# Batched attention-times-value: TensorE's program rewritten as a loop over units, with the spreading of v moved ahead of the unit's transposes

## The chip, the cores and the metric

The kernel runs on one NeuronCore of one Trainium2 chip. The metric is the device time of one execution in microseconds (us). A core has five engines with their own instruction streams: TensorE (PE, its weight loads are shown apart as PEld), VectorE (DVE), ScalarE (ACT), GpSimd (POOL) and SyncE (SP). They meet only at semaphores. Sixteen DMA engines move data between HBM and the on-chip memory; POOL and SP issue the transfers here. An engine's sequencer (PEq, SPq and so on in the profile) handles waits, branches and register arithmetic.

## The reference

```python
batch, n_heads, seq, head_dim = 8, 12, 1024, 64
...
def reference(attn_weights, v):
    return np.einsum('bhqs,bhsd->bhqd', attn_weights, v).astype(np.float32)
```

For each of 96 heads a 1024 x 1024 matrix of float32 is multiplied with a 1024 x 64 matrix. The sum runs over s, the last axis of `attn_weights`, while a matrix product on TensorE sums over partitions. So every block of `attn_weights` has to be transposed first.

## The kernel before

Heads are taken four at a time: q counts 24 such groups (`NV`). Partition 32h + p holds 32 query rows of head h of the group. Each group is cut into two units of 16 rows for each partition, so there are 48 units (`NU`); unit 2q + i lives in the buffer `abf[i]`, one of two. POOL loads a unit with one transfer that casts float32 to bf16 on the way (`load_attn`, L344). The load of unit n + 2 goes into the buffer of unit n, and POOL issues it once unit n's transposes are done. POOL also loads v for four groups at a time (`load_v`, L350), and stores part of the output in two bursts in mid-run and one at the end (L358); SP stores the last groups. All of POOL's transfers lie in one software queue in the order of their issue.

TensorE does four things for a unit:

- 16 groups (g) of four transposes each (`transpose_g`, L144) into four PSUM banks in turn. VectorE and ScalarE copy a group to `at` (`copy_g`, L277), ten groups by VectorE and six by ScalarE. Group g waits for the copy of group g - 4 (`s_cp`); the second eight wait for `s_half`, which SP raises and which holds units back only behind the bursts of stores and, in the last two units, until the second half of the load has landed.
- In even units, the spread (`spread_v`, L161): 32 matmuls of 512 columns, eight for each of the group's four heads, with a 0/1 matrix as weights, which distribute v (`vr`) over the partitions in the order the product needs. They write all of `po` and `px`, four PSUM banks. VectorE and ScalarE copy them to `vbf` (`spread_copy`, L250). Head h has its v in 16 partitions, and the matmuls read a block of 32 partitions; heads 0 and 1 are in one block, 2 and 3 in another, and the heads are taken in pairs (0, 2) and (1, 3), matmul by matmul in turn.
- The transposes back of the unit before (`transpose_back`, L174, eight matmuls from `ot` into `px`), which ScalarE copies to `osb` (`back_copy`, L258).
- The product (`multiply`, L189): 64 matmuls into `po`, which VectorE and ScalarE copy to `ot` half each (`product`, L289).

The order on TensorE is written out by hand. Its loop has 24 turns of two units each, and the body holds the product twice, the transposes twice, the transposes back twice, and the spread four times, one copy for each place that v can have in `vr`, chosen by three branches. VectorE and ScalarE loop over four units. In `unit` the copies of the transposes stand first, then (even units) the two spread copies of the engine, then, on ScalarE, the copies back, then the product's copy.

SP waits at the start until both halves of the first v are there. The second half is issued by POOL behind the load of unit 0 (L367); SP's wait for it shows in the profile at L413. Then it raises `s_vr`, on which the spread waits.

Of the kernel before, what the change touches and what calls it, by code (L numbers as in the profile page):

```python
# [10 lines left out]
def kernel(  # L11
# [76 lines left out]
    def count_of(g):  # L88

        return sum(on_dve(x) == on_dve(g) for x in range(g + 1))  # L90

    PER_DVE = sum(on_dve(g) for g in range(G))
    PER_ACT = G - PER_DVE

# [27 lines left out]
    s_t = {True: sem("s_t_dve"), False: sem("s_t_act")}  # L122
# [4 lines left out]
    s_last, s_ot, s_vbf = sem("s_last"), sem("s_ot"), sem("s_vbf")  # L127
# [8 lines left out]
    with tc.tile_critical(sync_engine=mybir.EngineType.Pool, no_gpsimd_drain=True):  # L136
        pe = nc.tensor

        def transpose_g(a, g, n):
            if g >= 4:  # L140
                pe.wait_ge(s_cp[g - 4], n)
            words = a[:, g].bitcast(fp32).rearrange("p (c k) -> p k c", k=KW)
            for k in range(KW):
                last = pe.matmul(  # L144
                    out=pt[g % 4][:, k],
                    lhsT=words[:, k],
                    rhs=ident,
                    is_transpose=True,
                    start=(k == 0),
                    stop=(k == KW - 1),  # L150
                )
            last.then_inc(s_t[on_dve(g)])

        def spread_v(n, banks):

            for pair in ((0, 2), (1, 3)):
                for b in range(VB):
                    for h in pair:
                        j = n % 2 * VH + h
                        rows = ds(j * (P // V8) // VR * VR, VR)  # L160
                        last = pe.matmul(  # L161
                            out=banks[h],
                            lhsT=spread[rows, j, ds(VB - 1 - b, P)],
                            rhs=vr[rows, n // 2, b],
                            start=(b == 0),
                            stop=(b == VB - 1),
                        )
                        if b == VB - 1:
                            last.then_inc(s_sp)

        def transpose_back():
            for j0 in range(0, GH, 4):
                for j in range(4):
                    last = pe.matmul(  # L174
                        out=px[j0 // 4][:, ds(j * P, P)],
                        lhsT=ot[:, j0 + j],
                        rhs=ident,
                        is_transpose=True,
                        start=(j == 0),
                        stop=(j == 3),  # L180
                    )
                last.then_inc(s_back)

        def multiply(outs, h, half):

            n = 0
            for kw in range(KW):
                for par in range(2):
                    last = pe.matmul(  # L189
                        out=outs,  # L190
                        lhsT=vbf[:, 2 * kw + par, h],
                        rhs=at[:, ds(half * GH, GH), kw, ds(h * VP, VP), par],
                        start=(n == 0),
                        stop=(n == SB - 1),
                    )
                    n += 1
            return last

        def pe_unit(i, n, both, loaded, it):

            pe.wait_ge(*loaded)
            for g in range(G):
                if g == GH:
                    pe.wait_ge(s_half, n)
                transpose_g(abf[i], g, n)
            pe.wait_ge(s_ot, both)
            if i == 0:
                pe.wait_ge(s_vr, it)
                which = pe.snap((it - 1) % V_AT_ONCE)
                with pe.If(which > 1):  # L210
                    with pe.If(which > 2):
                        spread_v(3, po + px)
                    with pe.Else():
                        spread_v(2, po + px)
                with pe.Else():
                    with pe.If(which > 0):
                        spread_v(1, po + px)
                    with pe.Else():
                        spread_v(0, po + px)
                pe.wait_ge(s_vbf, it * 4)  # L220
            transpose_back()
            pe.wait_ge(s_last, both)
            for hp in range(2):
                for h in range(2):
                    for half in range(2):
                        outs = po[hp][ds(half * D, D), ds(h * GH * VP, GH * VP)]
                        last = multiply(outs, 2 * hp + h, half)
                last.then_inc(s_m)

        pe.wait_ge(s_const, 4)  # L230
        with nc.Fori(1, NV + 1, 1, engines=(PE,)) as it:
            loaded = pe.snap(it * 16)
            second = pe.snap(it * 2)
            first = pe.snap(second - 1)
            both = pe.snap(it * 4)
# [230 lines left out]
```

## Time and profile before

| | us |
|---|---|
| median of 3 runs (lowest to highest) | 1050.49 (1050.24 to 1050.53) |
| the profiled execution's own time | 1050.36 |
| its span, first to last instruction | 1049.0 |
| PE busy / DVE busy / ACT busy | 794.9 / 389.5 / 469.6 |
| PE idle ahead of the transposes (L144) | 211.2, of it 187.8 until a load of `abf` had landed |
| mean granted clock of TensorE | 0.875 of full speed |

The profiled execution is 0.13 us under the median, and 1.36 us of its time lie outside the span. In the profile, "busy" is the union of an engine's instructions; a row like "9.45 PE bank L144 x64" in the chain of waits is a piece of the path that ended last, with its start in front. In the timeline a row holds start, duration, engine, line, operation, output from inputs, count, and in brackets how long the engine was idle before and what released it. DMA share is the mean busy share of the 16 DMA engines; it is summed from whole packets, so a short stretch can read above 1.

### The profile page before, as it was taken

What the parts mean: (1) busy time and instruction counts of PE and PEld (TensorE: products, weight loads), DVE (VectorE), ACT (ScalarE), POOL (GpSimd) and SP (SyncE); (2) the same over time, 40 slices, a digit from 0 to 9 for tenths busy, and PEclk for the clock granted to TensorE, in tenths of its full rate; (3) what the DMA queues carried; (4) which work ended last, traced back from release to release, by engine and by line L of the source; (5) the groups of instructions that cost most, each with busy time, mean ns of one, the idle gap of its engine ahead of it and who ended that gap; (6) DMA issues with size and microseconds to landing.
All of it is one profiled execution on the core that took longest, in us unless ns stands there. A gap on an engine that the chain in (4) does not pass through costs nothing.

```text
span 1049.0 us, 17363 instructions
## 1 busy us (share of the span) xinstructions
PE 794.9 (76%) x7304; PEld 708.4 (68%) x7304; DVE 389.5 (37%) x584; ACT 469.6 (45%) x590; POOL 36.9 (4%) x68
## 2 busy tenths in 40 slices
PE   0978788479889393888949789758678884987994
PEld 0777687368778383777838688657667774867884
DVE  1443344234435151343515344323324332533542
ACT  0445355244545261354525455344435543544553
POOL 1000000000000000000000000000000000000000
PEclk9989799798999696889969899887878987998998
DMA  9999999999999999999999999999999999999999
GB/s 216 225 219 219 217 211 215 220 219 217 220 216 210 218 220 379 217 220 210 211 223 219 219 219 220 203 220 220 318 236 220 212 211 223 219 220 215 212 214 400
DMA packets 10662, 239.68 MB, mean 228 GB/s; under 512 B 1056, under 2 KB 1056, under 8 KB 1184
## 3 DMA queue, kind: packets, MB, share of 16 engines
q0 software_dynamic: 10080, 232.26, 98.9%
q1 hardware_dynamic: 576, 7.34, 1.7%
q8 instruction: 3, 0.05, 0.0%
q14 instruction: 3, 0.02, 0.0%
HBM read 427.82 MB, written 25.17 MB: 432 GB/s over the span
## 4 chain that ended last, share of the span: by engine, by line
DMA 71%; PE 26%; issue 1%; POOL 1%; ACT 0%; DVE 0%; ACTq 0%; SPq 0%; POOLq 0%
DMA abf<-in_attn_weights_dram 63%; PE bank L144 22%; DMA out_dram<-osb 8%; PE bank L161 3%; PE bank L189 1%; PE bank L174 0%; POOL vr L350 0%; ACT osb L258 0%; DVE osb L258 0%; ACT vbf L250 0%; POOL abf L344 0%; ACT ot L289 0%; POOL out_dram L358 0%; ACTq L258 0%; SPq L420 0%
## 5 line engine op out<-in xcount | busy, mean ns | idle before, releaser
L144 PE MATMUL bank<-ident,abf 128*128 128x128 f32 x3072 | 431.0, 308 | 211.2 <-DMA abf<-in_attn_weights_dram 187.8
L144 PEld LDWEIGHTS bank<-ident,abf 128*128 128x128 f32 x3072 | 421.3, 212 | 222.9 <-DMA abf<-in_attn_weights_dram 195.5
L277 DVE COPY at<-bank 128x1024 bf16<-128x1024 bf16 x480 | 319.7, 689 | 402.2 <-PE bank L144 395.5
L277 ACT COPY at<-bank 128x1024 bf16<-128x1024 bf16 x288 | 287.9, 1012 | 329.1 <-PE bank L144 329.1
L189 PE MATMUL bank<-at,vbf 128*64 128x256 bf16 x3072 | 225.2, 285 | 0.0
L189 PEld LDWEIGHTS bank<-at,vbf 128*64 128x64 bf16 x3072 | 203.4, 111 | 19.0 <-issue 6.1
L258 ACT COPY osb<-bank 64x512 f32 (+1 forms) x194 | 112.4, 580 | 28.2 <-PE bank L174 25.6
L289 DVE COPY ot<-bank 128x512 f32<-128x512 f32 x48 | 33.2, 692 | 207.1 <-PE bank L189 207.1
L161 PE MATMUL bank<-vr,spread 32*128 32x512 bf16 x768 | 87.0, 375 | 0.5 <-issue 0.2
L289 ACT COPY ot<-bank 128x512 f32<-128x512 f32 x48 | 28.1, 585 | 129.0 <-PE bank L189 129.0
L174 PE MATMUL bank<-ident,ot 128*128 128x128 f32 x392 | 61.6, 309 | 29.3 <-ACT vbf L250 28.7
L174 PEld LDWEIGHTS bank<-ident,ot 128*128 128x128 f32 x392 | 50.7, 158 | 41.4 <-ACT vbf L250 40.5
L161 PEld LDWEIGHTS bank<-vr,spread 32*128 32x128 bf16 x768 | 35.2, 93 | 43.9 <-issue 1.6
L250 ACT CAST vbf<-bank 128x512 bf16<-128x512 f32 x48 | 25.8, 589 | 74.3 <-PE bank L161 74.3
L344 POOL DMA_DIRECT2D abf<-in_attn_weights_dram x50 | 26.9, 537 | 814.8 <-PE bank L144 813.9
L250 DVE CAST vbf<-bank 128x512 bf16<-128x512 f32 x48 | 30.9, 686 | 29.0 <-PE bank L161 29.0
L277 ACT ACT_TABLE_LOAD x12 | 15.4, 1283 | 6.4 <-DMA osb<-in_v_dram 6.2
L350 POOL DMA_DIRECT2D vr<-in_v_dram x6 | 4.0, 674 | 134.6 <-PE bank L161 134.6
L358 POOL DMA_DIRECT2D out_dram<-osb x5 | 3.1, 620 | 7.5 <-ACT osb L258 7.5
L258 DVE COPY osb<-bank 64x512 f32<-64x512 f32 x2 | 1.4, 689 | 3.0 <-PE bank L174 3.0
L325 DVE MEMSET ident<- 128x128 f32 x1 | 0.2, 165 | 6.2 <-DMA osb<-in_v_dram 6.2
L332 DVE CAST vr<-osb 128x1024 bf16<-128x1024 f32 x2 | 2.2, 1138 | 0.0
(9 smaller groups left out, 5.1 us busy)
## 6 DMA issues: line engine op xcount, KB each, us to landing
abf<-in_attn_weights_dram POOLq DMA_DIRECT2D x46, 4096.0 KB, 29.1
vr<-in_v_dram POOLq DMA_DIRECT2D x5, 2048.0 KB, 15.8
out_dram<-osb POOLq DMA_DIRECT2D x1, 8192.0 KB, 39.4
abf<-in_attn_weights_dram POOLq DMA_DIRECT2D x4, 2048.0 KB, 22.9
out_dram<-osb POOLq DMA_DIRECT2D x3, 2048.0 KB, 32.9
out_dram<-osb SPq DMA_DIRECT2D x3, 2048.0 KB, 14.2
out_dram<-osb POOLq DMA_DIRECT2D x1, 4096.0 KB, 41.7
osb<-in_v_dram SPq DMA_DIRECT2D x1, 1024.0 KB, 5.1
```

The lines of the kernel that those rows point to most:

```text
L144: last = pe.matmul(out=pt[g % 4][:, k], lhsT=words[:, k], rhs=ident, is_transpose=True, start=(k == 0), stop=(k == KW - 1),)
L161: last = pe.matmul(out=banks[h], lhsT=spread[rows, j, ds(VB - 1 - b, P)], rhs=vr[rows, n // 2, b], start=(b == 0), stop=(b == VB - 1),)
L174: last = pe.matmul(out=px[j0 // 4][:, ds(j * P, P)], lhsT=ot[:, j0 + j], rhs=ident, is_transpose=True, start=(j == 0), stop=(j == 3),)
L189: last = pe.matmul(out=outs, lhsT=vbf[:, 2 * kw + par, h], rhs=at[:, ds(half * GH, GH), kw, ds(h * VP, VP), par], start=(n == 0), stop=(n ...
L250: copy(out=vbf[:, :, h], in_=ps.rearrange("p (k d) -> p k d", k=SB)).then_inc(s_vbf)
L258: last = copy(out=rows[ds(n // 2 % 2 * HP, HP), ds(pp * 2 * G + n % 2 * G, G)].rearrange("p (half j) d -> p j half d", half=2)[:, ds(4 * k ...
L277: ins = copy(out=at[:, g].rearrange("c k j two -> c (k j two)"), in_=bank[g % 4].bitcast(bf16),)
L289: copy(out=ot.rearrange("c j (pp h p) -> c h j pp p", pp=2, h=VH)[:, ds(2 * e, 2)], in_=po[e].rearrange("c (h j p pp) -> c h j pp p", h=2, ...
L332: last = nc.vector.tensor_copy(out=vr_first[:, 0, part], in_=v32[:, part])
L344: pool.dma_start(out=abf[n % 2][:, ds(g0, gn)].rearrange("p g s -> p (g s)"), in_=attn_q[n // 2][:, ds((n % 2 * G + g0) * S, gn * S)],).th ...
L350: pool.dma_start(out=vr[:, ds(q % V_AT_ONCE // 2, fours // 2)].rearrange("p n b x -> p n (b x)"), in_=v_n(q, fours),).then_inc(s_v, 16)
L358: eng.dma_start(out=out_n(q, fours), in_=at_slot, **({"single_packet": True} if eng is pool and fours == 2 else {}),).then_inc(done, 16)
```

## The change

TensorE now loops over units: 49 turns (`NU + 1`), each of which runs the product of the unit before, then the transposes of this unit, then the transposes back. The first turn has no product, the last no transposes. There is one copy of the product, one of the transposes back, and one of the transposes for each of the two buffers, chosen by a branch. What was the product at the end of a unit is now at the head of the next turn, so the order of transposes, transposes back and product is the same as before.

The spread stands in front of the even unit's transposes, after the product of the unit before, and has one copy: a loop over the four heads with eight matmuls in each turn, whose addresses come from registers (the bank, the head's place in `spread`, the half of `vr`). The matmuls read all 128 partitions, not a block of 32. The spread waits for both copies of the product before (`s_ot`), because it writes the same `po`; and the even unit's transposes wait in the program behind it. The last transposes of an even unit wait for the spread copies (`s_vbf`), instead of the transposes back.

PE, the end of an even unit's transposes and what followed, before (the rows `x32` are the copies of the spread):

```order
L144 MATMUL bank<-ident,abf 128x128 [waits s_cp11]
L144 MATMUL bank<-ident,abf 128x128 x3
L206 ISA
L210 ISA [waits s_vr,s_ot]
L210 COMPARE_AND_BRANCH
L211 COMPARE_AND_BRANCH
L161 MATMUL bank<-vr,spread 128x512 x32
```

The spread came after the last transposes of its unit (those that wait for `s_cp11`). Now, on PE, the start of an even unit:

```order
L153 UNCONDITIONAL_BRANCH [waits s_ot1,s_vr,s_ot0,s_const]
L153 ISA
L155 ISA x2
L155 MATMUL bank<-vr,spread 128x512
L155 ISA
L155 MATMUL bank<-vr,spread 128x512
L155 ISA
L155 MATMUL bank<-vr,spread 128x512
```

and the end of the spread's loop with the transposes behind it:

```order
L155 MATMUL bank<-vr,spread 128x512
L153 REGISTER_ALU
L153 COMPARE_AND_BRANCH
L210 ISA
L142 MATMUL bank<-ident,abf 128x128 [waits s_abf0]
L142 MATMUL bank<-ident,abf 128x128 x15
L142 MATMUL bank<-ident,abf 128x128 [waits s_cp0]
```

So the first transpose of an even unit (it waits for the load, `s_abf0`) now stands behind the spread, and each spread matmul behind a register instruction.

VectorE's loop has two units instead of four, and both engines' spread copies stand at the head of an even unit. VectorE, around the spread copies, before:

```order
L277 COPY at<-bank 128x1024 [waits s_t_dve]
L249 ISA
L250 CAST vbf<-bank 128x8x64 [waits s_sp] x2
L288 REGISTER_ALU
L289 COPY ot<-bank 128x2x16x16 [waits s_m]
```

and now:

```order
L287 ISA
L227 CAST vbf<-bank 128x8x64 [waits s_sp]
L226 REGISTER_ALU
L227 CAST vbf<-bank 128x8x64 [waits s_sp]
L253 REGISTER_ALU
L254 COPY at<-bank 128x1024 [waits s_t0]
L254 COPY at<-bank 128x1024 [waits s_t2]
```

The two casts went from behind the unit's last copy to ahead of its first. The semaphores for transposed groups are counted by bank (`s_t0` to `s_t3`) rather than by copying engine. POOL issues the same transfers in the same order; it waits for `s_t3`, which the last group raises, and for the spread's count.

```diff
-    bank = [nc.alloc_psum_tensor(f"bank{i}", [P, 512], fp32).ap() for i in range(8)]
-    pt = [b.rearrange("p (k j) -> p k j", k=KW) for b in bank[:4]]
-    po = bank[4:6]
-    px = bank[6:8]
+    bank = nc.alloc_psum_tensor("bank", [P, 8, 512], fp32).ap()
+    pt = [bank[:, i].rearrange("p (k j) -> p k j", k=KW) for i in range(4)]
+    po, px = (bank[:, ds(i, 2)] for i in (4, 6))
...
+        def transposes(i, n):
+            for g in range(G):
+                if g >= 4:
+                    pe.wait_ge(s_cp[g - 4], n)
+                words = abf[i][:, g].bitcast(fp32).rearrange("p (c k) -> p k c", k=KW)
+                for k in range(KW):
+                    if g == GH - 1 and k == KW - 1:
+                        pe.wait_ge(s_half, n)
+                    if i == 0 and g == G - 1 and k in (1, 2):
+                        pe.wait_ge(s_vbf[k - 1], n)
+                    last = pe.matmul(
...
+                last.then_inc(s_t[g % 4])
-        def spread_v(n, banks):
-
-            for pair in ((0, 2), (1, 3)):
+        def spread_v(j0, part):
+            with nc.Fori(0, VH, 1, engines=(PE,)) as h:
                 for b in range(VB):
-                    for h in pair:
-                        j = n % 2 * VH + h
-                        rows = ds(j * (P // V8) // VR * VR, VR)
-                        last = pe.matmul(
-                            out=banks[h],
-                            lhsT=spread[rows, j, ds(VB - 1 - b, P)],
-                            rhs=vr[rows, n // 2, b],
...
+                    last = pe.matmul(
+                        out=bank[:, ds(h + 4, 1)].rearrange("p one x -> p (one x)"),
+                        lhsT=spread[:, ds(h + j0, 1), ds(VB - 1 - b, P)].rearrange(
+                            "p one x -> p (one x)"
+                        ),
+                        rhs=vr[:, ds(part, 1), b].rearrange("p one x -> p (one x)"),
+                        start=(b == 0),
+                        stop=(b == VB - 1),
+                    )
+                last.then_inc(s_sp, 2)
...
+        def multiply(it):
+            for h in range(VH):
+                for half in range(2):
...
+                            if h == 0 and (half, n) in ((0, SB - 1), (1, 0)):
+                                pe.wait_ge(s_last[half], it)
...
+        def step(it):
+            with pe.If(it > 1):
+                multiply(it)
+            with pe.If(it < NU + 1):
+                with pe.If(pe.snap(it % 2) < 1):
+                    pe.wait_ge(s_abf[1], pe.snap(it * 8))
+                    transposes(1, it)
                 with pe.Else():
...
+                    pe.wait_ge(s_const, 4)
+                    for e in range(2):
+                        pe.wait_ge(s_ot[e], it)
+                    pe.wait_ge(s_vr, it)
+                    spread_v(pe.snap(it // 2 % 2 * VH), pe.snap(it // 4 % 2))
+                    pe.wait_ge(s_abf[0], pe.snap(it * 8 + 8))
+                    transposes(0, it)
+            for e in range(2):
+                pe.wait_ge(s_ot[e], it)
             transpose_back()
...
+        with nc.Fori(1, NU + 2, 1, engines=(PE,)) as it:
+            step(it)
...
+                now = [base + (4 * n + c) for c in range(9)]
+                if n % 2 == 0:
+                    spread_copy(e, po[:, e], now[2 * e + 2])
+                    spread_copy(2 + e, px[:, e], now[2 * e + 6]).then_inc(s_vbf[e], 2)
                 for g in mine:
-                    copy_g(g, of_t + (n * per + count_of(g)))
-                if n % 2 == 0:
-                    spread_copy(e, po[e], of_sp + (2 * n + 2 * e + 2))
-                    spread_copy(2 + e, px[e], of_sp + (2 * n + 2 * e + 2))
+                    copy_g(g, now[g // 4 + 1])
...
-            un = 4
+            un = 2 if dve else 4
...
-                pool.wait_ge(s_sp, 4 * (q + 1))
+                pool.wait_ge(s_sp, 8 * (q + 1))
                 load_v(q + 1, V_LOADS[q + 1])
-            pool.wait_ge(s_t[True], (n + 1) * PER_DVE)
+            pool.wait_ge(s_t[3], 4 * (n + 1))
             load_attn(n + 2)
```

More of the change, by code (lines that the diff above doesn't have):

```diff
@@ L120 @@
     s_held = sem("s_held")
-    s_t = {True: sem("s_t_dve"), False: sem("s_t_act")}
+    s_t = [sem(f"s_t{b}") for b in range(4)]
     s_sp, s_m = sem("s_sp"), sem("s_m")
@@ L137 @@
         pe = nc.tensor
[L139 to L152, printed above, removed]
@@ L181, in transpose_back @@
                     )
[L182 to L197, printed above, removed]
@@ L230 @@
[L230 to L235, printed above, removed]
-            pe_unit(0, first, pe.snap(both - 2), (s_abf[0], loaded), it)
-            pe_unit(1, second, both, (s_abf[1], loaded), it)
-        pe.wait_ge(s_ot, 2 * (NU + 1))
-        transpose_back()
+                last.then_inc(s_back, 2)
+        def multiply(it):
+            for h in range(VH):
+                for half in range(2):
+                    n = 0
+                    for kw in range(KW):
+                        for par in range(2):
+                            if h == 0 and (half, n) in ((0, SB - 1), (1, 0)):
+                                pe.wait_ge(s_last[half], it)
+                            last = pe.matmul(
+                                out=po[ds(half * D, D), h // 2, ts(h % 2, GH * VP)],
+                                lhsT=vbf[:, 2 * kw + par, h],
+                                rhs=at[:, ds(half * GH, GH), kw, ds(h * VP, VP), par],
+                                start=(n == 0),
+                                stop=(n == SB - 1),
+                            )
+                            n += 1
+                last.then_inc(s_m)
```

86 lines of the change are left out of this document (29 added, 57 removed).

## The prediction

> **What bounds the kernel now.** I read the page's parts on the DMA queues first, then the costliest groups, then the windows cut at places where the DMA rate changes, and last the timeline at both ends.
>
> ```profile
> DMA  9999999999999999999999999999999999999999
> ...
> q0 software_dynamic: 10080, 232.26, 98.9%
> q1 hardware_dynamic: 576, 7.34, 1.7%
> q8 instruction: 3, 0.05, 0.0%
> ...
> L144 PE MATMUL bank<-ident,abf 128*128 128x128 f32 x3072 | 431.0, 308 | 211.2 <-DMA abf<-in_attn_weights_dram 187.8
> ```
>
> ```profile
> 0.00:4.70 4.70, 0.00 (x0) 0.00 (x0) 0.00 (x0) 0.00 (x0) 1.95 (x7) 1.00 0.61 202
> 4.70:25.00 20.30, 0.00 (x0) 0.00 (x0) 4.20 (x6) 1.28 (x1) 2.25 (x2) 1.00 1.01 219
> 25.00:48.00 23.00, 20.53 (x168) 17.26 (x168) 8.62 (x13) 9.99 (x13) 0.58 (x1) 0.93 1.04 223
> 48.00:400.00 352.00, 273.96 (x2568) 245.20 (x2568) 135.06 (x203) 164.95 (x207) 11.73 (x21) 0.89 1.01 217
> 400.00:1022.00 622.00, 487.91 (x4441) 434.49 (x4442) 233.88 (x351) 284.17 (x357) 20.37 (x37) 0.86 1.01 228
> 1022.00:1047.00 25.00, 12.46 (x129) 11.48 (x127) 7.71 (x12) 9.15 (x13) 0.00 (x0) 0.86 0.99 418
> 1047.00:1049.00 2.00, 0.00 (x0) 0.00 (x0) 0.00 (x0) 0.00 (x0) 0.00 (x0) 0.50 0.18 74
> ```
>
> Columns of the windows: stretch, its length, busy time of PE, PEld, DVE, ACT and POOL, granted clock, DMA share, GB/s. The DMA share is about 1 from 4.7 to 1047 us: in loads at 217 to 228 GB/s, at the end in stores at 418. The software queue alone is busy for 98.9% of the span. PE idles 211.2 us ahead of the transposes, 187.8 of it for a load. So the time is 4.7 us, plus the bytes at these rates, plus 2 us. The change moves no bytes, so TensorE can only matter where it lets the queue run dry, or at the two ends.
>
> The queue runs dry if the load of unit n + 2, issued after unit n's transposes, comes later than the last data of load n + 1. The steady pace:
>
> ```profile
> 88.20 7.95 PE L144 MATMUL bank<-ident,abf 128*128 128x128 f32 x64
> 95.99 1.04 PE L174 MATMUL bank<-ident,ot 128*128 128x128 f32 x8
> 96.95 4.48 PE L189 MATMUL bank<-at,vbf 128*64 128x256 bf16 x64
> 110.74 9.81 PE L144 MATMUL bank<-ident,abf 128*128 128x128 f32 x64 [9.30 <-DMA abf<-in_attn_weights_dram]
> ...
> 149.35 9.34 PE L144 MATMUL bank<-ident,abf 128*128 128x128 f32 x64 [3.81 <-DMA abf<-in_attn_weights_dram]
> ```
>
> Two loads take 149.35 - 110.74 = 38.6 us, 19.3 each. A unit without its spread takes 96.95 + 4.48 - 88.20 = 13.2 us on PE when it starts without a pause, and transposes after a pause take 9.3 to 9.8 us instead of 7.95.
>
> **The spread's price.** It loses its pairs.
>
> ```profile
> L161 PE MATMUL bank<-vr,spread 32*128 32x512 bf16 x768 | 87.0, 375 | 0.5 <-issue 0.2
> ...
> L210 PEldq FUSED_REGOPS  x24: 67/69/80, 34.5 to 1009.1; - x24
> ...
> L231 PEldq COMPARE_BRANCH  x24: 67/208/218, 60.0 to 1032.7; - x24
> ```
>
> 768 matmuls fill 87.0 us, 113 ns each, while one of them lasts 375 ns: they overlap. Two neighbours lie in different blocks of partitions and write different banks, so I read 113 as half of a 227 ns step of a pair. Matmuls over all 128 partitions that add into one bank have no such neighbour. The trace has none of 512 columns. Bounds: 113 ns (3.6 us for a spread, if pairing gave nothing) and 375 ns (12.0 us, no overlap at all). I take 227 ns, 7.3 us, since it is one pass of 512 columns in the same trace. A register instruction of 69 ns ahead of each hides under 227. The loop's four branches of 0.2 us hide in PE's queue: at PE's old loop end the next transposes start after 0.20 us of idle, no later than where there is no branch (the row at 88.20 has no gap at all).
>
> The Trainium skill speaks against this part: its page "TensorE: Matmul & The Clock Gate", section "Why this matters for your kernels", says that a matmul over 32 partitions takes as long as one over 128 and that the gain is in running several row blocks at once. That gain is what the change gives up, and the 113 ns agree with it. The same page (Part 1) gives 215.7 ns for 512 columns at full clock; by that a spread is an estimated 6.9 us, and the sum below comes out 0.4 us earlier at the first load.
>
> **Steady state: nothing.** An odd unit now is followed by the spread before the even unit's transposes. The spread waits for ScalarE's copy of the product:
>
> ```profile
> 1034.79 1.09 PE L174 MATMUL bank<-ident,ot 128*128 128x128 f32 x8 [0.68 <-ACT ot L289]
> ...
> 76.58 3.63 PE L161 MATMUL bank<-vr,spread 32*128 32x512 bf16 x32
> ...
> 80.27 1.07 ACT L250 CAST vbf<-bank 128x512 bf16<-128x512 f32 x2 [3.07 <-PE bank L161]
> 80.53 0.53 POOL L350 DMA_DIRECT2D vr<-in_v_dram  x1 [23.57 <-PE bank L161]
> 81.06 0.54 POOL L344 DMA_DIRECT2D abf<-in_attn_weights_dram  x1
> 81.40 1.56 PEld L174 LDWEIGHTS bank<-ident,ot 128*128 128x128 f32 x8 [1.68 <-ACT vbf L250]
> ```
>
> From an odd load's landing PE needs 13.2 + 0.7 + 0.4 (a branch, three register instructions) + 7.3 = 21.6 us to the even transposes, 29.6 to their end; with a slow start of the odd ones (1.9) 31.5. The next landing is due at 38.6. So POOL issues the load 7 us before the queue needs it, where it had about 10: covered. Per pair PE needs 2 x 13.2 + 1.1 + 7.3 = 34.8 of 38.6 us. If this cover goes, the queue stops once in each pair.
>
> What else moves is free by the same cover. PE's wait for `vbf` (last row, 1.68 us for PEld) goes; next is the wait for the load. The spread copies now stand ahead of the transposes' copies; at the spread's end ScalarE has one left (0.53 us), and the second group, its first, needs two groups' time, 1.0 us. POOL's load of v (six times) was issued after the spread and held back the load of `abf` by 4.4 us (81.06 against 76.6, where the transposes had ended and the spread began); now v goes out while the transposes run, and the queue's order is the same. VectorE's twelve more loop ends cost some 0.1 us each on an engine busy 37%.
>
> **The start: here it is decided.**
>
> ```profile
> 0.74 0.38 SPq L134 DMA_DIRECT2D osb<-in_v_dram  x1
> ...
> 1.33 0.67 POOL L344 DMA_DIRECT2D abf<-in_attn_weights_dram  x1 [0.89 <-POOLq L450]
> 2.00 0.55 POOL L367 DMA_DIRECT2D vr<-in_v_dram  x1
> ...
> 25.20 9.90 PE L144 MATMUL bank<-ident,abf 128*128 128x128 f32 x64 [25.20 <-DMA abf<-in_attn_weights_dram]
> ...
> 35.40 0.58 POOL L344 DMA_DIRECT2D abf<-in_attn_weights_dram  x1 [25.23 <-PE bank L144]
> ...
> 48.19 2.07 PE L144 MATMUL bank<-ident,abf 128*128 128x128 f32 x15 [1.03 <-DMA abf<-in_attn_weights_dram]
> ```
>
> ```profile
> L413 SPq EVENT_SEMAPHORE  x1: 16884/16884/16884, 10.7 to 10.7; - x1
> ```
>
> Unit 0's transposes began at 25.20, when load 0 had landed. Now the first spread stands ahead, and its v lands behind load 0: SP's wait ends at 10.7 + 16.9 = 27.6. Branch and register instructions: 28.0. The spread starts on an idle PE; the first transposes took 9.90 instead of 7.95, so I add 2.0 to 7.3: it ends at 37.3. The transposes then run warm, 7.95: 45.2. POOL issues load 2 some 0.3 later (35.40 against 35.10 before): 45.5, 10.1 us later than before. Load 1 had landed at 48.2. The margin is 2.7 us, and in it the new load must get its first data moving.
>
> ```profile
> 1.00:1.50 0.50, 0.00 (x0) 0.00 (x0) 0.00 (x0) 0.00 (x0) 0.17 (x1) 1.00 0.00 0
> 1.50:2.00 0.50, 0.00 (x0) 0.00 (x0) 0.00 (x0) 0.00 (x0) 0.50 (x2) 1.00 1.02 180
> ...
> 4.50:5.00 0.50, 0.00 (x0) 0.00 (x0) 0.00 (x0) 0.00 (x0) 0.00 (x0) 1.00 3.15 819
> ```
>
> SP's transfer (0.74) moves data from 1.5 to 2.0 on: 0.8 to 1.3 us. POOL's first (1.33) was there at the latest when the rate jumped at about 4.7: 3.4 us. With 0.8 to 1.3 first data flow at 46.3 to 46.8, ahead of the landing by 1.4 or more, and the queue does not stop; with 3.4 they flow at 48.9, a stop of 0.7. I take the middle, 0.4 us. Bounds: a spread at 113 ns leaves 6 us of margin, stop 0; at 375 ns plus 3.4 us first data come at 53.7, a stop of 5.5. A stop is paid in full, since nothing later has slack in the queue.
>
> **The end.**
>
> ```profile
> 1024.72 4.11 PE L144 MATMUL bank<-ident,abf 128*128 128x128 f32 x32 [0.75 <-SPq L426]
> 1024.79 12.88 SPq L358 DMA_DIRECT2D out_dram<-osb  x3
> ...
> 1037.34 0.33 SPq L358 DMA_DIRECT2D out_dram<-osb  x1
> ```
>
> After the last load five stores of 2.1 MB remain; at 418 GB/s they fill the 25 us to 1047. The four earlier ones last to about 1042, and the last is issued at 1037.3. So PE may be up to some 3 us later there for nothing. It gets one transpose more after the last landing (0.12) and two branches (0.4).
>
> **Sum.** 1050.36 + 0.4 + 0 = 1050.8; the profiled execution is 0.13 under the median: 1050.9. A gain can hardly exceed 1.2 us: the queue never stops, and the shorter program saves at most the three instruction packets, each 0.05 MB / 3 = 17 KB, or 1.2 us on one DMA engine (219 / 16 GB/s), which a load waits for if it is the last one.
>
> **Rivals.** (1) Slower, the other side: the first spread is dearer or POOL's first data later, and the queue stops before load 2. Each us by which the transposes end later than 46.6 (44.5, if POOL's first data take 3.4 us) costs one; 0.2% (2.1 us, about what a measurement of this kernel can tell from no change) is reached 2.1 us after that. With 300 ns a matmul (register addresses) they end at 47.6, and with 3.4 us of delay the queue stops for 3.1: 1053.6; the bound is 1056.0. For it: the thin margin; against: 227 ns and SP's delay. (2) The spread is so dear in every pair that PE becomes the bound. Five loads of v (9.6 us each) lengthen the mean pair to 40.6, so the spread must exceed 40.6 - 27.5 = 13.1 us, 410 ns a matmul, over the 375 that one lasted. At half clock, 14.5 us, it would cost 1.4 a pair, some 30 us: 1080. Against: it directly follows the product, so the clock should be up. (3) The branches over unused copies fetch code again and again. With two fetches of 17 KB in each of 49 turns, 1.7 MB at 219 GB/s, the queue would take 7.6 us more: 1058.5. Against: the loop before jumped back 24 times over a longer body, and the whole run has 3 instruction packets.
>
> The Trainium skill, "Runtime: NRT & Kernel Launch", "Instruction fetch mechanics", states the rule behind (3): a taken branch out of the two pages held forces a fetch. The trace of before does not bear it out for PE (3 packets).
>
> **Numbers.** Forecast, the queue stays fed or nearly (1049.6 to 1052.6): 0.64. Rival 1: 0.25, of it 0.16 up to 1054.5. Rivals 2 and 3: 0.04 each. Something that gains over 0.2%, of which I see no sign: 0.03. The range 1049.6 to 1054.5 holds 0.80. Within 0.2%: 0.64; slower 0.25 + 0.08 = 0.33; faster 0.03.
>
> **What would show it.** In the profile after: DMA share about 1 throughout; spread matmuls about 227 ns apart; the first spread from 28.0 to 37.3; POOL's third load at 45.5 and no dent in the DMA rate around 47 to 50; PE idle for loads smaller by some 90 us. Wrong would be: a spread over 9.3 us in mid-run, a gap at 47, more than a few instruction packets.

## The result and the profile after

The changed kernel takes 1052.82 us (median of 11 runs, 1052.17 to 1054.07) against 1050.28 us (1049.93 to 1050.56) on the same chip: 1.0025 times as long, 95% interval 1.0016 to 1.0035. It is slower by 0.25%, or 2.5 us. That is the first rival of the prediction: the queue stops before load 2. The profiled execution took 1052.48 us (span 1051.0), 2.1 us over the profiled one of before.

The page after, its DMA row, the packets that fetch instructions, and the two groups that the prediction spoke of:

```profile
DMA  9999999999999999999999999999999999999999
...
q8 instruction: 1, 0.02, 0.0%
...
L142 PE MATMUL bank<-ident,abf 128*128 128x128 f32 x3072 | 414.2, 300 | 108.6 <-DMA abf<-in_attn_weights_dram 92.7
...
L155 PE MATMUL bank<-vr,spread 128*128 x768 | 183.2, 383 | 81.3 <-SPq L392 29.2
```

And the line of the engines' busy time:

```profile
PE 849.1 (81%) x7304; PEld 720.5 (69%) x7304; DVE 391.1 (37%) x584; ACT 471.3 (45%) x590; POOL 36.9 (4%) x68
```

TensorE's idle time ahead of the transposes fell from 211.2 to 108.6 us (for loads from 187.8 to 92.7), but 81.3 us of idle time now lie ahead of the spread, where 0.5 lay before. The spread fills 183.2 us where it filled 87.0. TensorE as a whole is busy for 849.1 us instead of 794.9, since its other work takes less time, at a mean granted clock of 0.938 instead of 0.875. So 54 us more of work went into idle time, and the total moved by 2.5. The DMA row is full in all 40 slices, since a slice is 26 us long and the loss is small. A finer cut shows it. Windows of after (columns as in the prediction: PE, PEld, DVE, ACT, POOL, clock, DMA share, GB/s):

```profile
44.00:56.00 12.00, 12.00 (x129) 11.52 (x128) 6.41 (x10) 7.70 (x11) 0.57 (x1) 1.00 0.94 191
...
48.50:400.00 351.50, 298.58 (x2608) 254.66 (x2605) 136.44 (x204) 166.22 (x209) 11.75 (x21) 0.95 1.01 216
400.00:1022.00 622.00, 514.25 (x4384) 435.64 (x4384) 233.02 (x348) 283.45 (x355) 20.36 (x37) 0.93 1.01 228
...
1026.00:1049.00 23.00, 12.97 (x136) 12.22 (x134) 8.16 (x13) 9.97 (x13) 0.00 (x0) 0.87 1.00 427
```

The same first window in before:

```profile
44.00:56.00 12.00, 10.97 (x115) 10.62 (x111) 6.61 (x10) 5.85 (x7) 0.00 (x0) 1.00 1.00 214
```

From 48.5 us on the rates are those of before. In the 12 us around load 2's start the queue moves 191 GB/s instead of 214: at 217 GB/s the missing 23 x 12 are 1.3 us. A packet is booked where it starts, so such a short window is good to some tenths of a microsecond. The single packets say it more closely: over the 16 DMA engines load 2 lands 1.6 us later than before on average, and this shift stays (1.6 to 1.8) to the last load.

The chain of waits at the start of after, the wait of SP in it, and the issue of load 2:

```profile
2.00 26.34 DMA vr<-in_v_dram
28.34 0.02 SPq L392
28.36 0.87 issue
29.23 8.66 PE bank L155 x32
37.89 7.68 PE bank L142 x64
```

```profile
L392 SPq EVENT_SEMAPHORE  x1: 17483/17483/17483, 10.9 to 10.9; - x1
```

```profile
45.87 0.57 POOL L321 DMA_DIRECT2D abf<-in_attn_weights_dram  x1 [35.57 <-PE bank L142]
```

V lands at 28.4, the spread runs from 29.2 to 37.9, the transposes to 45.6, and POOL issues load 2 at 45.87. Half-microsecond windows of after show when its first data flow:

```profile
46.50:47.00 0.50, 0.50 (x8) 0.49 (x9) 0.00 (x0) 0.49 (x2) 0.00 (x0) 1.00 0.01 0
47.00:47.50 0.50, 0.50 (x12) 0.48 (x10) 0.00 (x0) 0.49 (x2) 0.00 (x0) 1.00 4.65 786
```

The new packets begin at about 47.2, some 1.3 us after the issue. Load 1's last packets had ended on most of the 16 engines between 45.8 and 46.6. So those engines stood still for 0.6 to 1.4 us, and the first packet of each then took 0.4 to 0.9 us longer than the steady 2.43.

### The profile page after: what moved, and what is told of

The parts are those of the page before. It is cut to its first block, busy times and chain, and to the rows that moved or that the text cites. A ratio compares the mean times of both kernels' runs of the same rounds, so it can differ in the third digit from the quotient of the medians.

```text
span 1051.0 us, 18301 instructions
## 1 busy us (share of the span) xinstructions
PE 849.1 (81%) x7304; PEld 720.5 (69%) x7304; DVE 391.1 (37%) x584; ACT 471.3 (45%) x590; POOL 36.9 (4%) x68
## 2 busy tenths in 40 slices
DMA packets 10659, 239.64 MB, mean 228 GB/s; under 512 B 1056, under 2 KB 1056, under 8 KB 1184
## 4 chain that ended last, share of the span: by engine, by line
DMA 72%; PE 25%; issue 1%; DVE 0%; ACT 0%; POOL 0%; POOLq 0%; SPq 0%
DMA abf<-in_attn_weights_dram 70%; PE bank L142 22%; DMA vr<-in_v_dram 3%; PE bank L187 2%; PE bank L155 2%; PE bank L169 0%; DVE osb L235 0%; ACT ot L266 0%; POOL abf L321 0%; SPq L392 0%; POOLq L429 0%; POOLq L129 0%
## 5 line engine op out<-in xcount | busy, mean ns | idle before, releaser
L142 PE MATMUL bank<-ident,abf 128*128 128x128 f32 x3072 | 414.2, 300 | 108.6 <-DMA abf<-in_attn_weights_dram 92.7
L142 PEld LDWEIGHTS bank<-ident,abf 128*128 128x128 f32 x3072 | 408.2, 211 | 120.7 <-DMA abf<-in_attn_weights_dram 101.6
L155 PE MATMUL bank<-vr,spread 128*128 x768 | 183.2, 383 | 81.3 <-SPq L392 29.2
L187 PE MATMUL bank<-at,vbf 128*64 128x256 bf16 x3072 | 215.1, 278 | 0.0
L187 PEld LDWEIGHTS bank<-at,vbf 128*64 128x64 bf16 x3072 | 196.8, 108 | 13.3 <-issue 8.0
L155 PEld LDWEIGHTS bank<-vr,spread 128*128 x768 | 75.0, 98 | 184.0 <-issue 122.9
L227 ACT CAST vbf<-bank 128x512 bf16<-128x512 f32 x48 | 28.1, 585 | 216.5 <-PE bank L155 216.5
L227 DVE CAST vbf<-bank 128x512 bf16<-128x512 f32 x48 | 33.2, 692 | 217.2 <-PE bank L155 217.2
L169 PE MATMUL bank<-ident,ot 128*128 128x128 f32 x392 | 50.8, 273 | 0.8 <-ACT ot L266 0.8
L169 PEld LDWEIGHTS bank<-ident,ot 128*128 128x128 f32 x392 | 44.8, 142 | 1.0 <-issue 1.0
## 6 DMA issues: line engine op xcount, KB each, us to landing
out_dram<-osb POOLq DMA_DIRECT2D x1, 8192.0 KB, 45.8
```

Source lines behind the costliest of these rows:

```text
L142: last = pe.matmul(out=pt[g % 4][:, k], lhsT=words[:, k], rhs=ident, is_transpose=True, start=(k == 0), stop=(k == KW - 1),)
L155: last = pe.matmul(out=bank[:, ds(h + 4, 1)].rearrange("p one x -> p (one x)"), lhsT=spread[:, ds(h + j0, 1), ds(VB - 1 - b, P)].rearrange ...
L169: last = pe.matmul(out=px[:, j0 // 4, ds(j * P, P)], lhsT=ot[:, j0 + j], rhs=ident, is_transpose=True, start=(j == 0), stop=(j == 3),)
L187: last = pe.matmul(out=po[ds(half * D, D), h // 2, ts(h % 2, GH * VP)], lhsT=vbf[:, 2 * kw + par, h], rhs=at[:, ds(half * GH, GH), kw, ds( ...
L227: return copy(out=vbf[:, :, h], in_=ps.rearrange("p (k d) -> p k d", k=SB))
```

## The experiments

**Theory S** says that the 2.5 us are lost once, at the start: the first spread waits for a v that lands behind load 0, so unit 0's transposes free their buffer too late for load 2. Its rival **P** says that they are lost a little in every pair of units, since the looped spread takes TensorE longer. The code and the second loop of VectorE are the remaining parts. Each ratio below is against the kernel before, run on the same chip.

**The first v ahead of load 0 (after).** The only edit is the order of two issues of POOL:

```diff
-        load_attn(0)
         pool.dma_start(out=vr_first[:, 1], in_=v_first[:, 1]).then_inc(s_v0, 16)
+        load_attn(0)
```

> The changed kernel, with one edit: POOL issues the second half of the first v ahead of load 0, not behind it. Theory S (the whole loss is the stop of the DMA queue between load 1 and load 2, at 46 to 47.4 us, because the first spread stands ahead of unit 0's transposes and its v lands late): the first spread runs while load 0 is still coming, unit 0's transposes start at about 28 us and end at about 37, POOL issues load 2 before 39, the queue does not stop: 1050.1 to 1050.6, against 1050.3 before and 1052.8 changed. Theory P (the loss is paid a little in every pair of units, by the spread that takes 8.4 us instead of 3.6): no change, 1052.8.

Measured: 1050.59 us (1050.37 to 1051.06), 1.0004 of before (0.9995 to 1.0013). Its timeline at the start:

```profile
11.89 3.19 PE L155 MATMUL bank<-vr,spread 128*128 x7 [11.89 <-issue]
...
28.54 9.77 PE L142 MATMUL bank<-ident,abf 128*128 128x128 f32 x64 [7.85 <-DMA abf<-in_attn_weights_dram]
...
38.61 0.57 POOL L321 DMA_DIRECT2D abf<-in_attn_weights_dram  x1 [28.59 <-PE bank L142]
```

And its window of load 2's start:

```profile
44.00:56.00 12.00, 8.16 (x48) 8.16 (x49) 4.29 (x7) 3.96 (x5) 0.00 (x0) 0.72 1.00 216
```

The spread now runs while load 0 is still on its way, the transposes start as soon as load 0 is there, load 2 is issued at 38.61, and the queue moves 216 GB/s. Every other part of the change is still in the kernel, the looped spread and the looped product included. S stands, and P falls: what is left beside the start is within 0.2%.

**The same edit in before**, as a control:

> The kernel before with the second half of the first v ahead of load 0 in POOL's order, as a control for that edit: unit 0's transposes start 2.4 us later (27.6), load 2 is issued at about 37.9, still 8 us before load 1 ends. Theory S (only a stop of the queue costs): 1050.0 to 1050.6. If the edit gains by itself, below 1049.9, and the cure of the changed kernel would be no cure of its stop.

Measured: 1050.16 us (1049.92 to 1050.8), 1.0002 (0.9993 to 1.0011). Alone the edit gains nothing. In the changed kernel it takes away a loss.

**The old paired spread in the new place.** The four written-out copies of before, chosen by a branch, stand where the change has its loop (and the engines that copy the spread wait for the paired counts):

```diff
-                    spread_v(pe.snap(it // 2 % 2 * VH), pe.snap(it // 4 % 2))
+                    which = pe.snap(it // 2 % V_AT_ONCE)
+                    with pe.If(which > 1):
+                        with pe.If(which > 2):
+                            spread_v(3)
...
```

> The changed kernel with the spread's old form in its new place: four written-out copies, 32 partitions a matmul, heads in pairs (0, 2) and (1, 3); VectorE's and ScalarE's spread copies wait for their pair as before. Theory S: the first spread takes about 3.6 us plus some 2 for the slow clock instead of 8.7, so unit 0's transposes end at about 42.5, load 2 is issued at 42.8, first data 1.4 us later at 44.2, ahead of the end of load 1 (45.8): no stop, 1050.2 to 1050.8. Rival Q (the place in front alone costs it, by the wait for the product's copies in every pair): 1052 to 1053.

Measured: 1052.86 us (1051.81 to 1053.63), 1.0025 (1.0015 to 1.0035). The expectation missed. The start of its timeline, and its window:

```profile
29.58 7.01 PE L158 MATMUL bank<-vr,spread 32*128 32x512 bf16 x32 [29.58 <-issue]
...
36.52 9.77 PE L142 MATMUL bank<-ident,abf 128*128 128x128 f32 x64
...
46.59 0.57 POOL L333 DMA_DIRECT2D abf<-in_attn_weights_dram  x1 [36.13 <-PE bank L142]
```

```profile
44.00:56.00 12.00, 12.00 (x129) 11.52 (x128) 6.31 (x10) 8.13 (x11) 0.57 (x1) 1.00 0.83 167
```

I had expected the paired spread to save half its time there. In the kernel before it takes 3.63 us in mid-run (the prediction's row at 76.58), here on an engine that had waited 7.01, and the transposes behind it still take the 9.77 us of a slow start. What the shorter spread saves (8.66 to 7.01) the transposes give back (7.68 to 9.77). Load 2 is issued at 46.59, and the rate falls to 167 GB/s. So the place of the spread costs the time with either form of it, and the lost pairs cost nothing measurable here.

The first spread is not alone in this. The second spread of this run, the transposes behind it, and a window over the later part of both:

```profile
66.17 5.14 PE L158 MATMUL bank<-vr,spread 32*128 32x512 bf16 x32 [1.43 <-ACT ot L278]
71.24 9.50 PE L142 MATMUL bank<-ident,abf 128*128 128x128 f32 x64
```

```profile
68.20:74.90 6.70, 6.70 (x33) 4.58 (x30) 2.60 (x4) 2.09 (x3) 0.53 (x1) 0.50 0.84 181
```

Two microseconds into the paired spread the granted clock falls to 0.50. In the later units of this kernel the spread takes 3.6 to 6.3 us. The mean granted clock of the run is 0.852, against 0.938 in after, whose spread reads 128 rows.

**The same with the first v ahead of load 0:**

> The changed kernel with the spread's old form (pairs, four copies) in the new place, which took 1052.9, and with the second half of the first v ahead of load 0 in POOL's order. Theory S: that loss too was the stop before load 2 (its first spread took 7.0 us on a slow clock and the transposes behind it 9.8), and it goes: 1050.1 to 1050.7. Rival Q (the place in front costs by itself in later units): 1052 to 1053.

Measured: 1050.54 us (1050.09 to 1050.84), 1.0001 (0.9992 to 1.001). The loss goes with the start in this form too. The first spread again takes 7.01 us (from 14.86), so that this is no accident of one run.

**More work behind the first spread.** Sixteen matmuls of 512 columns on constant data go between spread and transposes, in the first turn alone. Their bank is overwritten by the transposes, so the output does not hang on them.

```diff
+                    with pe.If(it < 2):
+                        for _ in range(16):
+                            pe.matmul(out=bank[:, 0]...)
                     pe.wait_ge(s_abf[0], pe.snap(it * 8 + 8))
```

> The changed kernel with 16 more matmuls of 512 columns (constant data, their output is overwritten), about 3.5 us, between the first spread and unit 0's transposes, in the first turn only. Theory S (the queue has already run dry before load 2, and from there each us costs one): the stop grows by 3.5 us, 1056.3, between 1055.8 and 1056.8. Theory P (the loss is paid in every pair of units): 3.5 us of one turn are hidden as before, 1052.8.

Measured: 1056.33 us (1055.55 to 1056.84), 1.0057 (1.0043 to 1.007), that is 3.5 us above after. Timeline and window:

```profile
38.50 3.64 PE L212 MATMUL bank<-spread 128*128 128x512 bf16 x16
...
50.12 0.57 POOL L330 DMA_DIRECT2D abf<-in_attn_weights_dram  x1 [39.90 <-PE bank L142]
```

```profile
44.00:56.00 12.00, 12.00 (x129) 11.52 (x128) 6.43 (x11) 8.02 (x11) 0.57 (x1) 1.00 0.54 102
```

3.64 us more on TensorE cost 3.5 us. In the profiled execution load 2 is issued 4.25 us later than in after (the first spread took 0.8 us longer there as well), and by the packets it lands 4.3 us later. At this place each microsecond is paid in full. The 112 GB/s that this window lacks against before are 6.2 us, beside 6.1 in the medians.

**The same work in the later pairs.** Eight such matmuls (1.9 us) in every even unit but the first; the edit is the same with `it > 2` and `range(8)`.

> The changed kernel with 8 such matmuls, about 1.7 us, between the spread and the transposes in all even units but the first: 23 x 1.7 = 39 us more work on TensorE. Theory S: POOL issues these loads some 6 us before the queue needs them, so nothing is lost: 1052.5 to 1053.2. Theory P (the queue or the end already pays for each us of a spread): about 1.7 us a pair, some 1090, or at least 1060.

Measured: 1057.97 us (1056.25 to 1060.01), 1.0071 (1.0057 to 1.0085). S had expected nearly nothing and P far more, so both missed. POOL's issue of one load in mid-run, in this kernel (first two rows from two timelines, then its window):

```profile
442.94 10.52 PE L142 MATMUL bank<-ident,abf 128*128 128x128 f32 x64 [7.67 <-DMA abf<-in_attn_weights_dram]
...
478.32 0.53 POOL L330 DMA_DIRECT2D abf<-in_attn_weights_dram  x1 [24.04 <-PE bank L142]
```

```profile
478.00:482.00 4.00, 4.00 (x59) 3.75 (x59) 1.29 (x2) 2.91 (x5) 0.53 (x1) 1.00 0.91 164
```

The same load in after, the odd unit ahead of it in the chain of waits, and its window:

```profile
473.94 0.53 POOL L321 DMA_DIRECT2D abf<-in_attn_weights_dram  x1 [22.28 <-PE bank L142]
```

```profile
440.99 9.86 PE bank L142 x64
```

```profile
478.00:482.00 4.00, 3.23 (x31) 2.94 (x28) 1.25 (x2) 1.63 (x3) 0.00 (x0) 1.00 1.22 262
```

From the packets I worked out how long before the first of the 16 engines ends the load ahead of it each load is issued. In after the smallest of these margins in mid-run are 3.6 to 4.8 us, at half a dozen places. In this kernel five fall to 0.7 to 2.1 us (0.7 at the row above), and by the packets the queue stops at them. So the steady state is covered, but by less than I had taken: 3.6 us, where I had allowed 1.9 us of new work as well within 6 to 7. The issue at this row moved by 4.4 us against after: 1.95 since the odd unit's load had itself landed later (442.94 against 440.99, the stops before it), 0.66 since the odd unit's transposes ran slower (10.52 against 9.86), and 1.9 for the added matmuls. The last two, 2.6, come off the margin, and so do some 1.2 of the 1.95: TensorE waits for the last engine to land its load, and the queue runs dry on the first. In after the engines end the load ahead of this one within 1.0 us (478.31 to 479.30), here within 2.2 (479.01 to 481.24), so that the first engine is only 0.7 us later and the margin falls by 3.7, from 4.4 to 0.7. Why the odd unit ran slower was not tested.

**A warm TensorE for the first spread.** Sixty-eight such matmuls ahead of the loop, while v is on its way:

```diff
+        pe.wait_ge(s_const, 4)
+        for _ in range(68):
+            pe.matmul(out=bank[:, 0]...)
         with nc.Fori(1, NU + 2, 1, engines=(PE,)) as it:
```

> The changed kernel with 68 more matmuls of 512 columns on constant data ahead of TensorE's loop, from about 10.5 us to about 27, while TensorE would wait for v; their output is overwritten. Theory S: the first spread runs at full clock, some 7.5 us instead of 8.7, load 2 is issued at about 44.5 and the stop shrinks from 1.4 to 0.3 us or none: 1050.5 to 1051.3; and since the slow clock's length differs from run to run, the runs lie closer together than the changed kernel's 1.9 us. Theory P: 1052.8.

Measured: 1052.91 us (1051.77 to 1053.59), 1.0025 (1.0016 to 1.0035): no gain. Timeline and window:

```profile
28.83 1.67 PE L155 MATMUL bank<-vr,spread 128*128 x7 [1.03 <-issue]
...
36.84 7.84 PE L142 MATMUL bank<-ident,abf 128*128 128x128 f32 x64
...
44.98 0.58 POOL L330 DMA_DIRECT2D abf<-in_attn_weights_dram  x1 [34.73 <-PE bank L142]
```

```profile
44.00:56.00 12.00, 12.00 (x128) 11.52 (x128) 6.43 (x10) 7.90 (x11) 0.58 (x1) 1.00 0.91 188
```

The spread takes 8.0 us from 28.83, and load 2 is issued 0.9 us earlier than in after; by S the time should have come down as much. The two readings of the stop disagree: by the window it is as in after (188 against 191 GB/s), by the mean landing of load 2, which does not hang on where a packet is booked, it shrank from 1.6 to 0.75 us. So at load 2 the earlier issue was worth its 0.9 us. Some 0.4 us were lost again to longer packets from 105 to 156 us, the last load still lands 0.5 us earlier than in after, and yet the two profiled executions end alike (1052.41 and 1052.48 us). What took the rest of the gain behind the last load stays open.

**Spread over all rows in the old place.** In before each matmul of the spread multiplies all 128 rows instead of the 32 that hold its v (the others are zeros in `spread`):

```diff
-                        rows = ds(j * (P // V8) // VR * VR, VR)
+                        rows = ds(0, P)
```

> The kernel before with one edit: each spread matmul reads all 128 partitions, so no two overlap; place, order and written-out copies as before. Theory S: the spread takes about 7 us instead of 3.6, behind the transposes and so behind POOL's load; nothing waits for it that the queue needs: 1050.1 to 1050.6. Theory P (the dearer spread itself costs, in every pair): 1052 to 1053.

Measured: 1058.13 us (1056.17 to 1060.05), 1.0081 (1.0067 to 1.0095). The expectation missed by 8 us. Its timeline around the first later load of v, and the window behind it:

```profile
76.79 7.08 PE L161 MATMUL bank<-vr,spread 128*128 128x512 bf16 x32
...
84.16 0.53 POOL L350 DMA_DIRECT2D vr<-in_v_dram  x1 [26.12 <-PE bank L161]
84.68 0.54 POOL L344 DMA_DIRECT2D abf<-in_attn_weights_dram  x1
```

```profile
84.00:88.00 4.00, 2.97 (x38) 2.75 (x39) 0.00 (x0) 3.13 (x6) 1.06 (x2) 1.00 0.67 96
```

The same window in before:

```profile
84.00:88.00 4.00, 4.00 (x62) 3.84 (x60) 0.69 (x1) 0.98 (x2) 0.00 (x0) 0.94 0.82 170
```

The spread takes 7.08 us instead of 3.63. In the six units that load v, POOL's program first waits for the spread, issues v, and only then the load of `abf`: both go out 3.6 us later (84.16 and 84.68 against 80.53 and 81.06), and the queue runs short. By the packets this load lands 1.4 us later than in before, and the shift grows to 4.2 at the last load. In before, v in these six units is issued 2.9 to 4.3 us before the first of the 16 engines ends the load ahead of it, the smallest margins in its mid-run, and 3.6 us use up most of that. The change itself widened them: in after v goes out 12 to 14 us ahead. That POOL's order costs the time was theory **V**, tested next.

**The same, with POOL's load of `abf` ahead of its wait for the spread:**

```diff
+            pool.wait_ge(s_t[True], (n + 1) * PER_DVE)
+            load_attn(n + 2)
             if i == 0 and q + 1 in V_LOADS:
                 pool.wait_ge(s_sp, 4 * (q + 1))
                 load_v(q + 1, V_LOADS[q + 1])
-            pool.wait_ge(s_t[True], (n + 1) * PER_DVE)
-            load_attn(n + 2)
```

> The kernel before with the spread over all 128 partitions (which took 1058.1), and one edit on POOL: in the six units in which it loads v, the load of the attention weights is issued first, when the transposes are done, and the load of v behind it, when the spread is done. Theory V (the 8 us of that kernel are lost because POOL waits for the dearer spread ahead of both loads, so that the queue runs dry once for each load of v): the loads come in time, 1050.1 to 1050.8. If the dearer spread itself costs: 1056 to 1060.

Measured: 1050.22 us (1050.04 to 1050.81), 1.0 (0.9991 to 1.0009).

```profile
L161 PE MATMUL bank<-vr,spread 128*128 128x512 bf16 x768 | 169.8, 379 | 4.9 <-SPq L423 4.4
```

That group from its page is the price of the lost pairs by itself: 169.8 / 768 = 221 ns of busy time a matmul, 7.08 us a spread, twice the 113 ns of before. The whole 83 us more cost nothing once no load waits behind them. The 8 us of the run before were POOL's order of waits.

**VectorE's loop over four units again (after):**

```diff
-            un = 2 if dve else 4
+            un = 4
```

> The changed kernel with VectorE's loop over four units again, the one part of the change not touched so far. Theory S: VectorE is busy 37% and waits for TensorE at each step, a loop end more or less changes nothing: 1052.2 to 1053.4, as the changed kernel. If VectorE's shorter loop costs: towards 1050.3.

Measured: 1052.99 us (1052.17 to 1054.0), 1.0026 (1.0016 to 1.0037), beside 1.0025 for after. This part of the change costs nothing that can be measured.

## Why the prediction was right in its mechanism and short in its sum

The forecast (queue fed or nearly, 1050.9), with a chance of 0.64, did not come; its first rival did, with a chance of 0.25 and 1052.82 at the lower edge of the 1052.6 to 1056 given there. The stated range, 1049.6 to 1054.5, holds the result because it covers most of that rival too. What the sum had wrong is the margin at load 2: it gave 2.7 us and a stop of 0.4, and the stop was 1.6. Step by step:

- **What bounds it:** right. DMA works throughout in both kernels, and nothing on TensorE counts but where the queue runs dry (with the first v ahead of load 0 the changed kernel is at 1.0004 of before, with all of TensorE's added work in it).
- **The place:** right. Each added microsecond at the first load costs one (3.5 us for 3.64).
- **When the spread starts:** 28.0 predicted, 29.23 measured. V landed at 28.4, not 27.6: SP's wait is 17.48 us, not 16.88, and begins 0.2 later. Between 11 and 14 us a packet that fetches instructions now runs among load 0's; before had none in its first 38 us (the last section shows that the longer wait goes with it). And 0.87 us lie between SP's signal and the first matmul, where I had taken 0.4 for a branch and the register instructions. This 1.2 us is the largest error on the way to the issue.
- **The spread's price:** 7.3 + 2.0 predicted, 8.66 measured. The matmuls are 0.217 us apart, not 0.227: eight are busy for 1.90 us (rows below), seven steps and 0.38 for the last one (a single one lasts 383 ns by the page's row). That makes 7.1 for 32 without a pause. The slow start on top was 1.6, not 2.0: the first eight are 0.43 apart (weight loads below). In mid-run a spread takes 8.2 to 8.3, 1.0 more than I took: between two turns of the loop 0.38 us are lost beyond a step (2.12 from turn to turn, where eight steps are 1.74), and I had put the loop's branches at nothing. In the first spread that loss does not show; there the branches had time to run ahead while the matmuls were slow, which is my reading and not tested.
- **The transposes and the issue:** they run warm, 7.68 against 7.95. Load 2 is issued at 45.87, 0.4 later than predicted.
- **The delay to first data:** I took the middle of bounds that gave a stop of 0 to 0.7 and so 0.4 us. The delay is 1.3 us, the upper end of SP's 0.8 to 1.3, and far from 3.4. But I let load 1 end at 48.2, its last engine's time, while most engines ran out at 45.8 to 46.6: each of the 16 engines has its own queue end, and I used the one that came last. This is the step that failed: it made a margin of 2.7 us, where from the issue at 45.87 there was 0.7 at most on these engines. With the slower first packets the stop is 1.6 us where the sum had 0.4. The Trainium skill, "DMA: Bandwidth & Descriptors", "Latency and other measured facts", gives about 1 us to the first byte for loads issued by GpSimd; the trace has 0.3 more, and neither alone gives the stop, which lies in the engines' uneven ends.
- **Steady state, nothing:** right in its outcome. The margin was 3.6 to 4.8 us at the tightest places, not 7. The gap between product and spread is 1.6 us instead of 1.1, and a spread is 8.3 instead of 7.3. Nor did before have about 10 us everywhere: in the six units that load v it had 2.9 to 4.3.

The weight loads of the first spread in after, and the steady pace, which carry the points on the spread:

```profile
31.76 0.15 PEld L155 LDWEIGHTS bank<-vr,spread 128*128 x1 [0.27 <-issue]
32.19 0.15 PEld L155 LDWEIGHTS bank<-vr,spread 128*128 x1 [0.27 <-issue]
32.55 4.85 PEld L155 LDWEIGHTS bank<-vr,spread 128*128 x23 [0.21 <-issue]
```

```profile
96.51 4.48 PE L187 MATMUL bank<-at,vbf 128*64 128x256 bf16 x64
102.57 1.90 PE L155 MATMUL bank<-vr,spread 128*128 x8 [1.58 <-ACT ot L266]
104.69 1.90 PE L155 MATMUL bank<-vr,spread 128*128 x8 [0.22 <-issue]
...
111.60 7.95 PE L142 MATMUL bank<-ident,abf 128*128 128x128 f32 x64 [0.76 <-DMA abf<-in_attn_weights_dram]
```

- **Rival 2 and rival 3** did not come: the spread's 8.3 us stay under 13.1, and there is one fetch packet by queue q8 in the whole run, where before had three. But that one comes at the wrong time (above), a cost of fetching that I had not put into the sum.
- **The end:** no loss shown. The rate there is 427 GB/s and the last transfer ends with the shift of the first stop.

About 1.6 to 1.8 us of the 2.1 between the two profiled executions are thus placed at load 2. The rest, 0.3 to 0.5 us, I have not placed.

## What to carry to other kernels

In a kernel whose DMA queue never stops, work moved onto another engine's path is free until it delays the issue that keeps the queue fed. So look for that issue at the start, where no earlier load has built a margin, and compare it with the first of the DMA engines to run out of work, not the last. When a step is moved ahead of a load's release, move the data that it needs ahead too, and look at what else stands behind its wait in the issuing engine's program.

## What the runs showed that I had not expected

- **A paired spread behind a pause of TensorE.** 32 matmuls over 32 rows take 7.01 us behind the long wait at the start, in both kernels that have them there, and 3.6 to 6.3 behind the pauses of later units, against 3.63 in mid-run of the kernel before, where they follow the transposes at once. The transposes directly behind the 7.01 take 9.77 us, as if nothing had run ahead; behind the spread over 128 rows they take 7.68. So the paired form left TensorE slow, and the full form did not: the granted clock falls to 0.50 within the paired spread shown above, and its mean is 0.852 and 0.855 in the two kernels, against 0.938 in after. Why the clock is granted so was not tested.
- **An empty queue restarts slowly.** 1.3 us pass from the issue of load 2 to first data, in after and in the five experiments whose queue stops there, and in after the first packets then take 2.85 to 3.34 us instead of 2.43.
- **A fetch of instructions shares the DMA engines with the loads.** Windowed to 11 to 14 us, the DMA view of after has it between the load's packets; 2.0% of 16 engines over 3 us is 0.96 us on one engine:

```profile
q0 software_dynamic: 16, 0.52, 81.5%
q8 instruction: 1, 0.02, 2.0%
```

  SP's wait for the v behind it is 0.6 us longer than before. The warm-up matmuls moved this packet to 29.2 us, behind v, and there SP's wait is as in before:

```profile
L401 SPq EVENT_SEMAPHORE  x1: 16914/16914/16914, 10.8 to 10.8; - x1
```

  Among the kernels with the first v behind load 0, the five whose packet runs at 12.2 to 12.5 us have waits of 17.31 to 17.57 us, and the four without a packet there (before, the two with all rows in the old place, and the warm one) 16.88 to 16.91. In after only the last of the 16 engines is late with v (28.34 us, the next at 27.75; in before the last two are at 27.59 and 27.60). So the packet delays one DMA engine, and SP waits for the last.
- **The scatter of the runs.** From the lowest to the highest, kernels whose queue stops spread over 1.3 us (more work behind the first spread) to 3.9 (all rows in the old place); the four experiments whose queue stays fed spread over 0.7 to 0.9. Before itself had single runs up to 1052.29 among some 25 beside the experiments, so this is a hint and no more.
